# Scan tiles laid out anew, stores moved to GpSimd's queue, the prefill's first two blocks paired, attention issued behind the last scan

## The chip, the cores and the metric

The kernel runs on one NeuronCore of a Trainium2 chip. Such a core has five engines, each with its own queue of instructions in fixed order: TensorE (PE: matrix products; PEld is its loading of weights), VectorE (DVE), ScalarE (ACT), GpSimd (POOL) and SyncE (SP, which here only issues DMA transfers). Sixteen DMA engines move data between the chip's memory and SBUF, the on-chip memory of 128 partitions; products land in the eight banks of PSUM. Engines wait for one another through semaphores. The metric is the device time of one launch in microseconds, the median over runs.

## The reference, cut to what matters

One layer of a diffusion backbone works on 128 context tokens and 1024 latent tokens (9 blocks of 128), width 1024. Attention (8 query heads of 64, 2 key and value heads) and an mLSTM matrix memory (4 heads of 128, scanned forward and backward in chunks of 128) read one input projection and are merged by one output projection; a SwiGLU FFN of width 2816 follows. Everything is float32.

```python
def trunk_layer(x, mods, ...):
    sh1, sc1, g1, sh2, sc2, g2 = mods            # from silu(cond) @ w_ada
    h = rmsnorm(x, norm1_w) * (1 + sc1) + sh1
    aq, ak, av, mq, mk, mv, mo, mg = split(h @ w_in)
    attn_o = attention(rope(norm(aq)), keys, vals)
    hm = mlstm_bidir(mq, mk * DK ** -0.5, mv, gates, init_f, init_b)
    hm = rmsnorm(hm, mlstm_norm_w) * sigmoid(mo)
    mix = concatenate([attn_o, hm]) @ w_out      # rows 0-511: attn_o, 512-1023: hm
    x = x + g1 * mix
    h2 = rmsnorm(x, norm2_w) * (1 + sc2) + sh2
    return x + g2 * ((silu(h2 @ w_g) * (h2 @ w_u)) @ w_down)

# one step of the scan, per head and chunk
s   = (q @ k.T) * exp(log_d - m_t)
num = s @ v + inter * (q @ C);  den = s.sum(-1) + inter * (q @ n)
h   = num / max(abs(den), exp(-m_t))
```

## The kernel before, in words

**Stages.** The nine blocks form three groups of three (CB = 3). (1) Modulations, norm 1, keys, values, gates and the query projection. (2) For each of the four mLSTM heads: `head_project` (its projections) with `head_mlstm` (the scan) of the head before woven in, and with attention on block group 0. (3) The scan of the last head, with no projection left beside it. Woven into it are `first`, which is the output projection's attention half for blocks 0 to 2 (`attn_out_first`, its results x1a stored to the memory tensors `x1a_d`), `ada`, which is the last modulation (`ada_rest`, two rows stored to `g_d`), and attention on group 1. (4) `prefill`: the output projection's other half, hm times w_out's rows 512 to 1023, for all nine blocks, and norm 2 of group 0. (5) The FFN, group by group, with the rest of attention on groups 1 and 2 woven in.

**Products.** A float32 product is done as three products of a high and a low part. `load_piece` (line 139) loads a 512 KB piece of weights into `raw` (line 151), ScalarE casts the high part `whi` (line 152), VectorE subtracts for the low part `wlo` (line 137). `out_block` (line 1142) makes 512 output columns of one block from 12 products (lines 1147 to 1149); a "half" below is one such call, n = 0 or 1, with two pieces of weights.

**The scan of one block.** `weights` makes scores and decay factors (lines 843 to 851), then come the products with the states (866), with the values (873), the division (876 to 884), hm (886, 887), its squares (889), and GpSimd's products (890, 896). For the last head, each three blocks are normalised together and stored to `hm_d[0]`, `hm_d[1]`, `hm_d[2]` (line 898): the first by SyncE, the other two by ScalarE's queue.

**Attention.** A unit is the turn of one block's queries (line 1008 on), one head (scores 1035, maximum 1037, exponential 1038, high and low part 1041 and 1042, two transposing DMAs on SyncE's queue, 1044 and 1045), or the value products of a pair of heads (1059, 1060). Group 1 has 39 units.

**What sets the order.** The stages are generators. `weave(main, side, n_main, n_side)` advances a side generator by n_side / n_main per unit of the main one; `beside` advances several at rates of their own. The instructions so listed go through a scheduler that simulates the engines and picks for each queue the ready instruction of highest priority; `hot(n)` lifts priority by n places. So an attention unit can be issued somewhat earlier than where it is listed. The order on each queue is then fixed.

**Where tiles lie.** Pools are stacked from both ends of SBUF; within a pool the tags lie in the order of their first allocation. A tile of a later stage that lies over tiles of an earlier one waits for these tiles' last users, tile by tile. In stage 3 the stack from one end is the weight pool (`ipair`, `iraw`: 4 buffers of 4 KB per partition each), hT0 to hT2 (12 KB each, used by `attn_out_first` as x1a, gta, mxa), the gate tiles and `mlp` (the scan's tiles, in the order of the lines headed `for tag, shape, bufs, dt`). In stage 4 the same end holds raw (2 buffers), whi (5) and wlo (5), over ipair, iraw, hT0 and the start of hT1, then x1 of groups 0 and 1, then aTh and aTl. From the other end, below attention's pools, come `ft` (gl, gx, t2), `fp` and `xp` (gx_all, mx), over the upper part of `mlp`.

**Prefill before.** For each block b: `load_x1(b + 1)`, `load_hm(b + 1)` (into t2), four transposes of hm, cast and subtraction to mx, half 0, half 1, for b < 3 the sums of squares (`stats`), for 0 < b <= 3 norm 2 of block b - 1. Attention on group 1 is advanced by 0.35 per yield. All four weight pieces of the stage are asked for ahead of the loop by `out_pieces(1)`.

## Time and profile before

| | us |
|---|---|
| median of 3 runs (lowest, highest) | 1570.68 (1569.95, 1571.53) |
| the profiled execution's own time | 1568.19 |
| its span, first to last instruction | 1566.4 |
| TensorE busy | 1484.4 |
| VectorE busy | 1017.7 |
| ScalarE busy | 771.7 |
| GpSimd busy | 267.8 |

How to read it: the profile is of one execution. In rows of groups the fields are line, engine, operation, written tile <- read tiles, shapes, count, then busy us and mean ns of one, then the idle time just before these instructions and what ended it. In rows by stretch of time each engine's busy us stands with its count, then TensorE's granted clock as a share of full speed, the share of the DMA engines and GB/s. In rows of the chain or in order of time the first number is the start and the second the length, in us; in brackets stand the idle time before and its releaser. SPq and ACTq are transfers issued on SyncE's and ScalarE's queues. Ends of TensorE's products are modelled, so neighbours overlap in their lengths; the distance of starts is the better measure.

### The profile page before, as it was taken

To read this page: it belongs to the slowest core of one execution; us is meant where nothing else is said; L and a number is where in the kernel's file an instruction comes from. 1 tells how busy PE (TensorE), PEld (TensorE's weight loads), DVE (VectorE), ACT (ScalarE), POOL (GpSimd) and SP (SyncE) were. 2 spreads that over 40 slices of the span, in tenths; PEclk is the share of its full clock that TensorE was granted. 3 is DMA by queue.
4 is the path that set the end of the run, shared out by engine and by line. 5 is a ranking of instruction groups with operands and counts; after the bars stand their busy time and mean duration, and the time that the engine had idled before them with its cause. 6 is when DMAs were issued, how large, how long until landed. Compare 5 with 4: busy or idle time off the path is not lost.

```text
span 1566.4 us, 23369 instructions
## 1 busy us (share of the span) xinstructions
PE 1484.4 (95%) x8539; PEld 1244.8 (79%) x8539; DVE 1017.7 (65%) x2007; ACT 771.7 (49%) x1413; POOL 267.8 (17%) x354
## 2 busy tenths in 40 slices
PE   6899999999999689999999999999999999999997
PEld 3544567677766468898998989989898989999996
DVE  4878554837669576677555677878866585554554
ACT  4754465847656344545432444556552443323333
POOL 0213333322343242100110101000010101001110
PEclk9899999999999799999999999999999999999999
DMA  9564323523657748767554547878773545534441
GB/s 362 177 190 156 100 68 41 130 38 68 122 148 170 254 80 201 182 182 170 153 154 144 152 126 237 195 172 178 176 169 114 168 129 175 162 117 139 148 139 63
DMA packets 387881, 236.91 MB, mean 151 GB/s; under 512 B 170198, under 2 KB 346790, under 8 KB 387766
## 3 DMA queue, kind: packets, MB, share of 16 engines
q1 hardware_dynamic: 385110, 231.84, 54.2%
q10 hardware_dynamic: 2656, 3.58, 1.1%
q8 instruction: 67, 1.10, 0.3%
q14 instruction: 48, 0.39, 0.1%
HBM read 183.79 MB, written 13.26 MB: 126 GB/s over the span
## 4 chain that ended last, share of the span: by engine, by line
PE 80%; DVE 9%; ACT 4%; DMA 4%; issue 2%; POOL 1%; SPq 0%; ACTq 0%; DVEq 0%; POOLq 0%
PE mm L1316 12%; PE mm L1317 11%; PE mm L1315 11%; PE mm L1115 5%; PE mm L1116 5%; PE mm L1117 5%; PE S L1035 4%; PE wi L485 3%; PE wi L484 3%; PE wi L483 3%; PE mm L1147 2%; PE mm L1148 1%; PE mm L1149 1%; PE mm L116 1%; PE po L1060 1%
## 5 line engine op out<-in xcount | busy, mean ns | idle before, releaser
L152 ACT CAST whi<-raw 128x1024 fp32r<-128x1024 f32 (+1 forms) x216 | 221.9, 1027 | 415.1 <-PE mm L1316 148.8
L137 DVE TENSOR_TENSOR wlo<-raw,whi 128x1024 fp32r<-128x1024 f32 (+1 forms) x216 | 259.9, 1203 | 204.9 <-ACT whi L152 204.4
L1316 PE MATMUL mm<-aTl,whi 128*128 128x384 f32 x1056 | 355.7, 337 | 2.7 <-DVE aTl L137 2.7
L1317 PE MATMUL mm<-aTh,wlo 128*128 128x384 f32 x1056 | 354.3, 336 | 0.0
L1315 PE MATMUL mm<-aTh,whi 128*128 128x384 f32 x1056 | 353.3, 336 | 0.0
L137 POOL TENSOR_TENSOR hl<-tn,hl 128x384 fp32r<-128x384 f32 x66 | 84.1, 1275 | 840.0 <-ACT hl L1338 757.3
L1316 PEld LDWEIGHTS mm<-aTl,whi 128*128 128x128 f32 x1056 | 198.5, 188 | 3.9 <-DVE aTl L137 3.3
L1315 PEld LDWEIGHTS mm<-aTh,whi 128*128 128x128 f32 x1056 | 198.1, 188 | 0.6
L1317 PEld LDWEIGHTS mm<-aTh,wlo 128*128 128x128 f32 x1056 | 198.4, 188 | 0.0
L1116 PE MATMUL mm<-wlo,hl 128*128 128x512 f32 x372 | 145.7, 392 | 0.0
L1115 PE MATMUL mm<-whi,hl 128*128 128x512 f32 x372 | 144.3, 392 | 0.0
L1117 PE MATMUL mm<-whi,hl 128*128 128x512 f32 x372 | 143.4, 392 | 0.0
L483 PE MATMUL wi<-ipair,hT 128*128 128x384 f16 (+2 forms) x408 | 135.2, 334 | 2.0 <-ACT hT L507 1.2
L484 PE MATMUL wi<-ipair,hT 128*128 128x384 f16 (+2 forms) x408 | 135.2, 334 | 0.0
L485 PE MATMUL wi<-ipair,hT 128*128 128x384 f16 (+2 forms) x408 | 132.0, 335 | 1.0 <-DVE hT L137 1.0
L1042 DVE SCALAR_TENSOR_TENSOR pl<-pr,st,ph 128x1152 f16<-128x1152 f32 (+1 forms) x72 | 94.8, 1317 | 33.9 <-ACT ph L1041 32.5
L1041 ACT ACTIVATE ph<-pr,st 128x1152 f16<-128x1152 f32 (+1 forms) x72 | 83.8, 1164 | 27.2 <-issue 7.2
L1037 DVE TENSOR_REDUCE st<-S 128x1 f32<-128x1152 f32 (+1 forms) x72 | 88.8, 1233 | 12.5 <-PE S L1035 12.3
L1038 ACT ACTIVATE pr<-S,st 128x1152 f32<-128x1152 f32 (+1 forms) x72 | 81.3, 1129 | 31.7 <-DVE st L1037 28.0
L1035 PE MATMUL S<-kst,qT 128*128 128x384 f32 (+1 forms) x400 | 86.8, 347 | 5.0 <-ACT pr L1038 5.0
L1104 DVE TENSOR_TENSOR t<-mm,gl 128x512 f32<-128x512 f32 x102 | 68.9, 685 | 26.2 <-DMA gl<-g_d 12.5
L1117 PEld LDWEIGHTS mm<-whi,hl 128*128 128x128 f32 x372 | 69.9, 188 | 14.2
(381 smaller groups left out, 2525.0 us busy)
## 6 DMA issues: line engine op xcount, KB each, us to landing
raw<-in_w_gu_dram SPq DMA_DIRECT2D x132, 512.0 KB
raw<-in_w_down_dram SPq DMA_DIRECT2D x60, 512.0 KB
a<-in_w_ada_dram SPq DMA_DIRECT2D x24, 512.0 KB
gl<-g_d SPq DMA_DIRECT2D x36, 256.0 KB
aw<-in_w_ada_dram SPq DMA_DIRECT2D x16, 512.0 KB
iraw<-in_w_in_dram SPq DMA_DIRECT2D x32, 256.0 KB
raw<-in_w_out_dram SPq DMA_DIRECT2D x12, 512.0 KB
x<-in_x_sample_dram SPq DMA_DIRECT2D x11, 512.0 KB
```

The source lines that it names most:

```text
L137: (dve if eng == "dve" else pool).tensor_tensor(out=out, in0=full, in1=hi, op=ALU.subtract)
L152: nc.scalar.copy(hi[:, :n], raw[:, :n])
L483: mm(ps[:, :n], ah, wh[:, k % 2, c0 : c0 + n], start=(k == 0), stop=False)
L484: mm(ps[:, :n], ah, wl[:, k % 2, c0 : c0 + n], start=False, stop=False)
L485: mm(ps[:, :n], al, wh[:, k % 2, c0 : c0 + n], start=False, stop=(k == KD - 1))
L1035: mm(S[:, n, 0:w], qT[:, h, :], kst[kv][:, t, c0 + n * w : c0 + (n + 1) * w], start=(t == 0), stop=(t == 1))
L1115: mm(ps, ah, wh[:, k % 2, :], start=(k == 0), stop=False)
L1116: mm(ps, ah, wl[:, k % 2, :], start=False, stop=False)
L1117: mm(ps, al, wh[:, k % 2, :], start=False, stop=(k == nk - 1))
L1315: mm(ps, wh[:, k, :], th[:, k, :], start=(k == 0), stop=False)
L1316: mm(ps, wh[:, k, :], tl[:, k, :], start=False, stop=False)
L1317: mm(ps, wl[:, k, :], th[:, k, :], start=False, stop=(k == KD - 1))
```

## The change

1. The tags of `mlp` are laid out in another order: hm, ssh, nu, it, ... first, and c0f, c0b, cs and qTm last.
2. In `attn_out_first`, x1a and mxa change places (hT2 and hT0); w_out's high and low pieces take the four `iraw` buffers, and `ipair` takes ada's two weight buffers, the raw piece and ada's row.
3. Stores by GpSimd's queue: the last head's `hm_d[1]` and `hm_d[2]`, each as three stores of one block, the three `x1a_d` stores, and ada's two rows to `g_d`.
4. In the last scan ada is advanced at 0.8 and `first` at 0.55 per yield (0.5 and 0.35 before). Attention on group 1 is no longer in the chain woven there (0.14 per yield, 37 yields); it is made after it and first advanced by the prefill.
5. The prefill loads hm of blocks 0 and 1 first, into buffers `hmr` of its own, then two weight pieces (n = 0), the gates and gx_all; x1 of blocks 0 and 1 and the two pieces for n = 1 are issued on SyncE's queue after gx_all (`tc.issue_after`). Blocks 0 and 1 are transposed together, then come both halves 0, then both halves 1, each with its block's end; from block 2 on the order is as before. mx has 3 buffers instead of 2, and `xp` is laid out as gx_all, hmr, mx.

```diff
-    def ada_rest(ns, silp, new_a4, new_part, new_row, early=2):
+    def ada_rest(ns, silp, new_a4, new_part, new_row, early=2, store=dma):
...
-            dma(g_d[0 if n == 2 else 1, :, j * 512 : (j + 1) * 512], row)
+            store(g_d[0 if n == 2 else 1, :, j * 512 : (j + 1) * 512], row)
...
-    for tag, shape, bufs, dt in (("cs", [P, P + 1], CSB, F32), ("c0f", [P, P + 1], 2, F32), ("c0b", [P, P + 1], 1, F32), ("hm", [P, NB, P], 2, F32), ("ssh", [P, NB], 2, F32), ("nu", [P, 2, P + 1], 4, F32),
-                                 ("it", [P, 2, P + 1], 3, F32), ("dn", [P, 2], 3, F32), ("jkh", [P, P], 1, BF16), ("sd", [P, 2, P], 4, F32),
-                                 ("dt", [P, 2, P], 4, F32), ("so", [P, P], 9, F32), ("va", [P, P + 1], 9, F32), ("kT", [P, P], 9, F32),
-                                 ("th", [P, P], 1, F32), ("qTm", [P, CT], 2 * NCH, F32), ("wv", [P, 2, P + 1], 2, F32), ("kt", [P, P], 2, F32)):
+    for tag, shape, bufs, dt in (("hm", [P, NB, P], 2, F32), ("ssh", [P, NB], 2, F32), ("nu", [P, 2, P + 1], 4, F32), ("it", [P, 2, P + 1], 3, F32),
+                                 ("dn", [P, 2], 3, F32), ("jkh", [P, P], 1, BF16), ("sd", [P, 2, P], 4, F32), ("dt", [P, 2, P], 4, F32),
+                                 ("so", [P, P], 9, F32), ("va", [P, P + 1], 9, F32), ("kT", [P, P], 9, F32), ("th", [P, P], 1, F32),
+                                 ("kt", [P, P], 2, F32), ("wv", [P, 2, P + 1], 2, F32), ("c0f", [P, P + 1], 2, F32), ("c0b", [P, P + 1], 1, F32),
+                                 ("cs", [P, P + 1], CSB, F32), ("qTm", [P, CT], 2 * NCH, F32)):
...
-                    (nc.scalar.dma_start if h == NH - 1 and c > 0 else dma)(hm_d[c][:, h * P : (h + 1) * P].rearrange("(b p) n -> p b n", p=P), hm[:, c * CB : (c + 1) * CB, :])
+                    cols = hm_d[c][:, h * P : (h + 1) * P]
+                    if alone and c > 0:
+                        for k in range(CB):
+                            nc.gpsimd.dma_start(cols[k * P : (k + 1) * P], hm[:, c * CB + k, :])
+                    else:
+                        dma(cols.rearrange("(b p) n -> p b n", p=P), hm[:, c * CB : (c + 1) * CB, :])
...
-        ahead = load_hm(0)
-        load_x1(0)
-        ws = out_pieces(1)
+        hms = [load_hm(0), load_hm(1)]
+        ws = [out_pieces(1, 0)]
         gs = out_gates()
-        gx_all = xp.tile([P, D], F32, name="gx_all")
-        dma(gx_all, g_d[0, 0:1, :].to_broadcast([P, D]))
+        gx_all = xp.tile([P, D], F32, name="gx_all", tag="gx_all")
+        with tc.issue_after(dma(gx_all, g_d[0, 0:1, :].to_broadcast([P, D])).ins):
+            load_x1(0)
+            load_x1(1)
+            ws.append(out_pieces(1, 1))
...
+        for b in range(2):
+            mix(b)
+            yield
+        for b in range(2):
+            half(b, 0)
+            yield
+        for b in range(2):
+            load_x1(b + 2)
+            half(b, 1)
+            yield
+            yield from end(b)
+        for b in range(2, NB):
+            load_x1(b + 2)
+            mix(b)
+            yield
+            for n in range(2):
+                half(b, n)
+                yield
+            yield from end(b)
...
-        x1 = hTp.tile([P, CB, D], F32, name="x1a", tag="hT0")
+        x1 = hTp.tile([P, CB, D], F32, name="x1a", tag="hT2")
         gt = hTp.tile([P, 6, 512], F32, name="gta", tag="hT1")
-        mx = hTp.tile([P, CB, NQ, P], F32R, name="mxa", tag="hT2")
-        ip = [wp.tile([P, 1024], F32R if i < 2 else F32, name=nm("ip"), tag="ipair", bufs=4) for i in range(4)]
-        ir = [wp.tile([P, 1024], F32R if i < 2 else F32, name=nm("ir"), tag="iraw", bufs=4) for i in range(4)]
+        mx = hTp.tile([P, CB, NQ, P], F32R, name="mxa", tag="hT0")
...
+        his, los = (ir[0], ir[1]), (ir[2], ir[3])
...
-                        dma(x1a_d[i], x1[:, i])
+                        nc.gpsimd.dma_start(x1a_d[i], x1[:, i])
...
-    oT = []
-    att = chain(att, attention(1, oT, set()))
-    weave(scan, beside((ada, 0.5), (first, 0.35), (att, 0.14)), 37, 37)
+    weave(scan, beside((ada, 0.8), (first, 0.55), (att, 0.14)), 37, 37)
     while len(done) < CB:
         next(att)
+    emit(att)
+    oT = []
+    att = attention(1, oT, set())
     emit(first)
```

`mix`, `half` and `end` are the former loop's three parts under names of their own; `out_pieces(half, n)` now returns the two pieces of one n.

More of the change, by code (lines that the diff above doesn't have):

```diff
@@ L1121, in three_blocks, with out_pieces @@
                 done(i, ps)
-    def out_pieces(half, own=None):
-        ws = []
-        for n in range(2):
-            pieces = []
-            for j in range(2):
-                r0 = half * 512 + 2 * j * P
-                rows = w_out[r0 : r0 + 2 * P, n * 512 : (n + 1) * 512].rearrange("(a p) n -> p a n", p=P)
-                pieces.append(load_piece([(full_view, rows)], (2, 512), raw=own and own[2], own=own))
-                own = None
-            ws.append(pieces)
-        return ws
+    def out_pieces(half, n):
+        pieces = []
+        for j in range(2):
+            r0 = half * 512 + 2 * j * P
+            rows = w_out[r0 : r0 + 2 * P, n * 512 : (n + 1) * 512].rearrange("(a p) n -> p a n", p=P)
+            pieces.append(load_piece([(full_view, rows)], (2, 512)))
+        return pieces
     def out_gates():
@@ L1202, in prefill @@
-            if c == 0:
+            cs = slice(n * 512, (n + 1) * 512)
+            ps = out_block(ws, n, *mixed[b])
+            g = gx[n] if b == 0 else gs[n]
+            if c < 2:
+                add_gated(x1s[c][i], ps, g, n, pool)
+            else:
+                xt = t2()
+                dma(xt, xrow(b)[:, cs])
+                t = t2()
+                dve.tensor_tensor(out=t, in0=ps, in1=g, op=ALU.mult)
+                pool.tensor_tensor(out=xt, in0=xt, in1=t, op=ALU.add)
+                dma(x1_d[i][:, cs], xt)
```

47 lines of the change are left out of this document (20 added, 27 removed).

## Prediction

> **What bounds the kernel now.** I read the page first (busy shares, the 40 slices), then the busy time by stretch around the one slice in which TensorE falls to 6 tenths, then the chain in order of time through that place, then what each queue issued there.
>
> ```profile
> span 1566.4 us, 23369 instructions
> PE 1484.4 (95%) x8539; PEld 1244.8 (79%) x8539; DVE 1017.7 (65%) x2007; ACT 771.7 (49%) x1413; POOL 267.8 (17%) x354
> PE   6899999999999689999999999999999999999997
> PE 80%; DVE 9%; ACT 4%; DMA 4%; issue 2%; POOL 1%; SPq 0%; ACTq 0%; DVEq 0%; POOLq 0%
> ```
>
> TensorE is busy 95% of the span and carries 80% of the chain. So what counts is where it idles or runs at a lowered clock; work that is only carried to another place costs its own length there and saves it here. The 14th slice (509 to 548 us) is the worst after the start. It is the passage from the last mLSTM scan to the prefill, which is what the diff touches.
>
> ```profile
> core 0: us, PE busy (x) PEld busy (x) DVE busy (x) ACT busy (x) POOL busy (x), PEclk, DMA share, GB/s
> 450.00:460.00 10.00, 7.05 (x42) 5.33 (x40) 7.46 (x21) 8.01 (x24) 6.93 (x9) 0.83 0.41 114
> 480.00:500.00 20.00, 18.79 (x124) 14.70 (x123) 19.19 (x58) 15.27 (x34) 6.40 (x7) 1.00 0.83 163
> 500.00:532.00 32.00, 17.94 (x75) 12.63 (x74) 19.53 (x43) 9.50 (x16) 6.25 (x6) 0.73 0.81 248
> 502.00:514.30 12.30, 8.38 (x46) 5.27 (x44) 10.56 (x29) 3.38 (x9) 5.20 (x5) 0.86 0.79 197
> 523.80:532.00 8.20, 7.53 (x20) 5.79 (x21) 3.34 (x4) 2.02 (x3) 0.00 (x0) 0.54 0.91 343
> 541.00:560.00 19.00, 12.87 (x74) 10.02 (x75) 15.62 (x42) 11.91 (x22) 7.09 (x5) 1.00 0.41 89
> 600.00:660.00 60.00, 56.24 (x325) 50.00 (x323) 39.56 (x52) 30.36 (x39) 12.44 (x9) 1.00 0.84 209
> ```
>
> TensorE's loss in this passage: idle 20 - 18.79 = 1.2 us and 32 - 17.94 = 14.1 us. To it comes work done at a lowered clock: 8.38 x (1 - 0.86) = 1.2 us and 7.53 x (1 - 0.54) = 3.5 us. Together **20.0 us**, the most that closing this hole alone can return. VectorE is full (19.19 of 20) before it. By the slices TensorE is at 9 tenths or more again from the 16th on (587 us), so anything moved there is paid there.
>
> ```profile
> 508.70 1.29 SPq L1044
> 510.10 1.29 SPq L1045
> 511.44 5.24 DMA raw<-in_w_out_dram
> 519.44 4.29 DMA t<-hm_d
> 455.85 0.90 PE L785 MATMUL mm<-wv,kt 128*128 128x258 f32 x2 [2.10 <-POOL wv L783]
> 498.95 0.61 PE L873 MATMUL wi<-va,sd 128*128 128x129 f32 x4
> 503.19 1.31 PE L1035 MATMUL S<-kst,qT 128*128 128x384 f32 x6
> 523.78 1.11 PE L116 MATMUL mm<-ident,t 128*128 128x128 f32 x4 [9.47 <-DMA t<-hm_d]
> ```
>
> The chain says why. The scan's last products run at 498.95, but SyncE's queue must first issue two attention transposes (508.70, 510.10), which wait for a softmax of attention on block group 1 that was woven into the scan. Only then come three weight loads, the third of them waiting for a buffer, and behind these, at 519.44, the load of the first hm block. TensorE waits 9.47 us for that load, and after it runs at clock 0.54.
>
> **The change, part by part.** *Attention behind the scan.* The scan yields 37 times; at 0.14 that drew five units of attention on group 1: the q turn and four heads. These now come with the prefill. The prefill draws as many units as before, so five more are left for the FFN.
>
> ```profile
> L1035 PE MATMUL S<-kst,qT 128*128 128x384 f32 x36 | 7.7, 350 | 0.0
> L116 PE MATMUL mm<-ident,qr 128*128 128x128 f32 x4 | 0.6, 272 | 0.0
> L1042 DVE SCALAR_TENSOR_TENSOR pl<-pr,st,ph 128x1152 f16<-128x1152 f32 x5 | 7.0, 1404 | 0.0
> L849 ACT ACTIVATE dt<-mm,QT 128x128 f32<-128x128 f32 x18 | 5.7, 365 | 3.6 <-PE mm L846 3.5
> L869 ACT ACTIVATE it<-wi,QT 128x129 f32<-128x129 f32 x16 | 5.1, 366 | 2.1 <-PE wi L866 2.1
> L886 ACT ACTIVATE hm<-nu,dn 128x128 f32<-128x128 f32 x9 | 3.5, 403 | 3.8 <-DVE dn L884 3.8
> L889 ACT ACTIVATE jkh<-hm 128x128 bf16<-128x128 f32 x10 | 3.1, 312 | 4.9 <-DVE hm L887 4.9
> L889 ACT ACTIVATION_READ_ACCUMULATOR jkh<-hm 128x1 f32 x10 | 1.9, 193 | 0.0
> 468.99 0.60 PE L866 MATMUL wi<-cs,qT 128*128 128x129 f32 x4
> 470.21 0.27 PE L846 MATMUL mm<-NM,selb 128*128 128x256 bf16 x1
> ```
>
> TensorE's part of the five units is 4 x 1.3 + 0.6 = 5.8 us; it is moved, not saved, and counts in neither direction. VectorE loses at least 4 x 1.40 = 5.6 us (L1042 alone) in the scan, where it was full. SyncE loses eight transposes of about 1.3 us, which will stand between weight loads of the FFN. What does cost: in 600 to 660 TensorE idles 60 - 56.24 = 3.8 us while the 23 units then left begin (39 less 5 and 11); if all of that is attention's, five more are **+0.8 us** (0 to 2).
>
> *Side work at 0.8 and 0.55.* The last modulation and the first half of the out projection now end after some 24 of the 37 yields instead of at the end. That frees the buffers under the new weights early, but the last 13 yields, 3.25 blocks, are scan alone. A block's products take 468.99 to 470.48, 1.5 us of TensorE; ScalarE needs 2 x 0.365 + 2 x 0.366 + 0.40 + 0.31 + 0.19 = 2.4 us. At ScalarE's pace TensorE idles 3.25 x 0.9 = **2.9 us**. Ends: 0, if prefill's transposes and halves fill in; 10.7 us at the old pace (from the last projection product at 455.85 to 498.95, 43.1 us for nine blocks, 4.8 each, 3.25 x 3.3). I take ScalarE's, since the old pace held attention and projection work too.
>
> *Layout.* Worked out from the tile sizes, the prefill's hm buffers now lie on kT, done with the last score product, no longer on t2 and rsqrt space; the low weight halves lie on mxa instead of on x1a, so they wait for the last projection product, not for x1a's stores. In exchange the x1 tile lies on x1a and so waits for all three of x1a's stores, and gx_all lies on va, free only after the scan's last product. This is what lets the hm load and the first two weight pieces be issued before the scan ends. Its price is in the next part.
>
> *Prefill paired, n=1 weights behind gx_all.* On SyncE the gx_all load must go out first, then two x1 loads, then the two n=1 pieces; attention's transposes queue behind them. None can start before va is free.
>
> ```profile
> 520.96 0.59 SPq L151 DMA_DIRECT2D raw<-in_w_out_dram  x1
> 522.11 0.65 SPq L1173 DMA_DIRECT2D gx_all<-g_d  x1
> 522.81 0.64 SPq L1166 DMA_DIRECT2D x<-x1a_d  x1
> 529.50 1.04 ACT L152 CAST whi<-raw 128x1024 fp32r<-128x1024 f32 x1 [3.98 <-DMA raw<-in_w_out_dram]
> 530.57 1.23 DVE L137 TENSOR_TENSOR wlo<-raw,whi 128x1024 fp32r<-128x1024 f32 x1 [4.34 <-ACT whi L152]
> 535.14 0.50 PE L1147 MATMUL mm<-whi,mx 128*128 128x512 f32 x1 [0.68 <-ACT mx L1184]
> 540.48 0.39 PE L1149 MATMUL mm<-whi,mx 128*128 128x512 f32 x1
> ```
>
> From the scan's last product to the first n=1 half: 0.65 + 2 x 0.64 + 0.59 issue, 8.5 landing (520.96 to 529.50), 1.04 cast, 1.23 subtract = 13.3 us. Cover on TensorE: the two n=0 halves, as long as block 1's two (535.14 to 540.87, 5.7 us), two transposed blocks (four transposes each as for the q turn, 1.2), and the q turn with two hoisted heads (3.2): 10.1 us. A new wait of **3.2 us** is left. Ends: 0 with the faster landing (511.44 plus 5.24 us), 6.4 without the heads. If the cover is gone altogether it is 13.3.
>
> *Clock.* A gap of 2.10 us at 455.85 lies in the stretch with clock 0.83: 7.05 x 0.17 = **1.2 us** for one more such gap (0 to 3.5, the loss after the long one). The Trainium skill, "TensorE: Matmul & The Clock Gate", Part 1, says that the clock halves after an idle window of about 3.4 us. By that, gaps of 3 us could go free and the sum would be 1.2 us better. The trace shows a lowered clock around 2.10 us.
>
> *Stores on GpSimd's queue.* Eleven: six pieces of hm in place of two stores on ScalarE's queue, three of x1a and two gate rows in place of five on SyncE's. The trace has none from GpSimd, so no price.
>
> ```profile
> 511.07 0.38 ACTq L898 DMA_DIRECT2D hm_d<-hm  x1
> 602.44 2.06 DMA x_d<-t
> ```
>
> The nearest issue row is 0.38 us; GpSimd is busy 6.25 us of 32, so 11 x 0.38 = 4.2 us hides, and I take nothing. The upper end is a store that holds the queue until it has landed, 2.06 us each. Behind it stand the hm products, the x1a sums and prefill's x1 sums, and SyncE's x1 load waits for the three x1a stores. A gain is possible too, as SyncE loses waits for GpSimd's sums; it stands in the hole already.
>
> **The sum.** 20.0 recovered, minus 2.9, 3.2, 1.2 and 0.8 = 8.1 left over: 11.9 us less. The profiled execution took 1568.19 us (span 1566.4 and 1.8 around it), so 1556.3 for it. The median of the runs, 1570.68, is 2.5 above that execution: **1559 us**. The likeliest's own range: the terms' ends hardly come together, so half of what they allow, 8.1 / 2 down and (7.8 + 3.2 + 2.3 + 1.2) / 2 up: 1555 to 1566.
>
> **The rivals.**
> *All of it closes* (15 in 100): the scheduler lays prefill halves into the scan's tail and the weights land in time. All 20 us go: 1551, and 1548 where half of the prefill's idle at 541 to 560 (19 - 12.87 = 6.1 us) goes too. For it: by the code the hm blocks 0 to 2 are stored when six blocks of the scan are still to come. Against: gx_all's wait on va.
>
> *The hole moves* (15 in 100): SyncE's queue, in order, waits at gx_all or x1, and the n=1 weights come 6 us later still. 11.9 - 6 = 5.9 us less: 1565. For it: the third and fourth weight loads cost just such waits now.
>
> *Attention was free filler* (7 in 100): the scan keeps its old pace to the end, 10.7 us idle in place of 2.9. 11.9 - 7.8 = 4.1 less, and with a second lowered clock (1.2) 2.9 less: 1568, no measurable change. Against: the chain's own steps at 508.70 and 510.10 are attention's.
>
> *GpSimd's queue becomes the bound* (13 in 100), the slower case: each store holds the queue for its landing. Three x1a stores, two rows and three hm pieces stand there in the last 25 us: 8 x 2.06 = 16.5 us, plus the sums between. The x1 load goes out that much later, with the n=1 weights behind it on SyncE. From 11.9 us of such delay the gain is gone; at 16.5 it is 4.6 slower: 1575. For it: VectorE and GpSimd are both at work there. Against: by the new rates x1a's sums end after some 20 of the 37 yields, and the time up to the scan's end may swallow most.
> The Trainium skill, "SBUF — State Buffer", "A bandwidth-pool intuition that's wrong", speaks against the change here: GpSimd writes the descriptors of its own stores and is locked out during some VectorE operations, with a store-like transfer of 620 ns becoming 3100. By an estimate from that figure eight stores would hold 25 us and the kernel would be 13 us slower. No trace here shows it.
>
> **How the numbers follow.** The likeliest has 50 in 100. A change under 0.2% (3.1 us) can't be told from none. Faster: 50 + 15 + 15 = 80; within 0.2%: 7; slower: 13. The range leaves out the far part of the first rival (some 8) and the far half of the last (6): 1549 to 1575.
>
> **What would show it.** Right: the wait for hm gone, SyncE issuing hm and the first weights before the scan's last product, no attention transposes between them, TensorE's clock near 1 through the passage, first FFN products about 18 us earlier than 611.9 (11.9 and the 5.8 moved).
> ```profile
> L1315 PE MATMUL mm<-aTh,whi x1056: 331/334/423, 611.9 to 1538.6; 128*128 128x384 f32 x176
> ```
> Wrong: a wait of over 10 us before the n=1 halves, GpSimd holding x1 sums, or TensorE idle within the scan in place of attention.

## The result, and the profile after

The changed kernel takes 1575.28 us (median of 18 runs, 1571.37 to 1582.65) against 1569.89 us of the kernel before in the same series: a ratio of 1.0037, 95% interval 1.0027 to 1.0046. It is slower, where I had forecast 1559 us and faster. Its profiled execution took 1571.5 us (span 1569.7), which is 3.8 below its own median; the one of before lies 1.7 below its median of 1569.89. So the two traces differ by 3.3 us and the medians by 5.4: some 2 us of the loss are not in this trace.

Lines have moved: 866 is now 867, 873 is 874, 898 is 902 and 904, 1147 to 1149 are 1149 to 1151, 1250 is 1278, 1161 is 1163, 1166 is 1168, 1035 is 1041, 869 is 870, 851 is 852, 1294 is 1322, 1315 is 1343.

From the page of the changed kernel: TensorE's 40 slices, and the chain's shares by engine.

```profile
PE   6799999999987699999999999999999999999997
...
PE 77%; DVE 9%; DMA 5%; ACT 5%; issue 2%; POOL 1%; SPq 0%; ACTq 0%; DVEq 0%; POOLq 0%
```

The dent in the slices has not gone. It was a 6 and an 8 (the 14th and 15th slice); it is now an 8, a 7 and a 6 (the 12th to the 14th), so it is longer and begins two slices earlier. Busy time by stretch, first of the kernel before, then of the changed one, shows this in us:

```profile
440.00:480.00 40.00, 36.85 (x246) 27.41 (x244) 27.77 (x74) 24.07 (x70) 16.87 (x23) 0.96 0.47 139
480.00:541.00 61.00, 44.92 (x233) 33.58 (x231) 43.73 (x112) 27.57 (x53) 16.52 (x16) 0.86 0.84 237
541.00:600.00 59.00, 50.01 (x261) 40.29 (x262) 43.32 (x92) 31.57 (x50) 21.94 (x16) 1.00 0.50 100
600.00:660.00 60.00, 56.24 (x325) 50.00 (x323) 39.56 (x52) 30.36 (x39) 12.44 (x9) 1.00 0.84 209
```

```profile
440.00:480.00 40.00, 32.38 (x204) 22.87 (x204) 20.05 (x62) 16.30 (x51) 12.46 (x20) 0.91 0.55 174
480.00:541.00 61.00, 38.91 (x210) 30.17 (x208) 40.54 (x117) 25.46 (x59) 25.11 (x29) 0.85 0.65 214
541.00:600.00 59.00, 53.91 (x277) 45.06 (x278) 44.62 (x86) 32.51 (x50) 22.63 (x16) 0.92 0.52 113
600.00:660.00 60.00, 58.72 (x324) 54.20 (x323) 33.96 (x45) 26.32 (x34) 10.49 (x8) 1.00 0.67 190
```

TensorE (first busy column) loses 36.85 - 32.38 = 4.5 us in 440 to 480 and 44.92 - 38.91 = 6.0 in 480 to 541, and takes back 3.9 and 2.5 behind that: 4.1 us less work by 660. All of the 10.5 lost ahead of 541 is idle time; up to 5.8 of it stands where attention's products stood, which were moved away on purpose, and the rest is new. The granted clock is lower too, 0.91 for 0.96 and 0.92 for 1.00.

What TensorE waited for in the passage (changed kernel, 440 to 700; total, times, longest):

```profile
PE mm L116 <- DMA hmr<-hm_d: 12.5, 1, 12.5
PE mm L116 <- ACT y L1322: 6.7, 1, 6.7
PE mm L116 <- ACT it L870: 3.9, 1, 3.9
PE mm L844 <- DVE sd L852: 2.6, 1, 2.6
```

The wait for hm, 9.47 us before, is 12.5. Three others are new or longer: 6.7 for norm 2's y (1.49 before the same transposes in the old trace), and 3.9 and 2.6 at the start of the last scan. The chain in order of time says what held hm (changed kernel):

```profile
502.35 0.60 POOL hm_d L902
502.95 1.57 issue
504.52 0.54 POOL hm_d L902
505.06 1.58 issue
506.64 0.54 POOL hm_d L902
507.18 1.57 issue
508.75 0.53 POOL x1a_d L1278
509.28 2.49 DMA g_d<-ip
511.86 4.16 DMA raw<-in_w_out_dram
```

GpSimd issues a store in 0.5 to 0.6 us, then stands 1.57 us before the next: 2.1 us a store, far from the 0.38 us row on which I had counted. The last gate row's store waits behind three stores of hm and one of x1a until 509.28. And SyncE waits for that row, since the second weight piece is loaded over it. SyncE's waits from 480 to 530 divide this wait, and SyncE's queue (start, length) shows what stood behind it:

```profile
SPq L151 <- DVE ip L453: 11.1, 1, 11.1
SPq L151 <- DMA g_d<-ip: 7.6, 1, 7.6
```
```profile
492.60 19.62 SPq L151 DMA_DIRECT2D raw<-in_w_out_dram  x2
512.27 0.93 SPq L1163 DMA_DIRECT2D hmr<-hm_d  x2
516.08 2.73 SPq L151 DMA_DIRECT2D raw<-in_w_out_dram  x2
```

The first piece goes out at 492.6, the second only at 511.86, and the hm loads, whose data was stored long before, stand behind it in the same queue. Of the second piece's wait 11.1 us pass until VectorE has finished the row (line 453), and 7.6 until its store has been issued and has landed. So the store on GpSimd's queue is the smaller part of this wait, and the larger is that ada's last row is finished so late.

### The profile page after: what moved, and what is told of

The parts are those of the page before. It is cut to its first block, busy times and chain, and to the rows that moved or that the text cites. A ratio compares the mean times of both kernels' runs of the same rounds, so it can differ in the third digit from the quotient of the medians.

```text
span 1569.7 us, 23407 instructions
## 1 busy us (share of the span) xinstructions
PE 1482.2 (94%) x8539; PEld 1248.4 (80%) x8539; DVE 1017.8 (65%) x2007; ACT 771.8 (49%) x1413; POOL 273.1 (17%) x365
## 4 chain that ended last, share of the span: by engine, by line
PE 77%; DVE 9%; DMA 5%; ACT 5%; issue 2%; POOL 1%; SPq 0%; ACTq 0%; DVEq 0%; POOLq 0%
PE mm L1344 11%; PE mm L1345 11%; PE mm L1343 11%; PE mm L1121 5%; PE mm L1122 5%; PE mm L1123 5%; PE S L1041 4%; PE wi L485 3%; PE wi L483 3%; PE wi L484 3%; PE po L1066 1%; PE mm L1151 1%; PE po L1065 1%; PE mm L1150 1%; PE mm L1149 1%
## 5 line engine op out<-in xcount | busy, mean ns | idle before, releaser
L1048 DVE SCALAR_TENSOR_TENSOR pl<-pr,st,ph 128x1152 f16<-128x1152 f32 (+1 forms) x72 | 98.7, 1371 | 32.3 <-ACT ph L1047 32.0
```

## The experiments

Medians and ratios are to the kernel before of the same series (1569.77 to 1570.18 us).

| run | edit | median, us | ratio (95%) |
|---|---|---|---|
| changed kernel | | 1575.28 | 1.0037 (1.0027 to 1.0046) |
| e1_row_apart | gate row in a buffer of its own | 1574.29 | 1.0028 (1.0015 to 1.0041) |
| e2_row_on_sync | gate rows stored by SyncE | 1574.22 | 1.0028 (1.0017 to 1.0038) |
| e3_ring | 2048 B for GpSimd's descriptors | 1571.80 | 1.0012 (1.0000 to 1.0024) |
| f1_row_ring | e1 and e3 (1024 B) | 1570.66 | 1.0005 (0.9994 to 1.0015) |
| e4_stores_back | all stores on their old queues | 1570.64 | 1.0000 (0.9991 to 1.0009) |
| h1_swap_only | projection's buffers as before | 1572.56 | 1.0015 (1.0002 to 1.0029) |
| f2_back_swap | e4 and h1 | 1568.33 | 0.9990 (0.9979 to 1.0001) |
| f3_ring_swap | e3 and h1 | 1565.01 | 0.9968 (0.9958 to 0.9977) |
| h2_hm2_gpsimd | f2, hm's last store on GpSimd | 1562.81 | 0.9959 (0.9942 to 0.9977) |
| e5_unpaired | blocks 0 and 1 not paired | 1577.74 | 1.0054 (1.0039 to 1.0069) |
| f6_ring_swap_unpair | f3, not paired | 1568.89 | 0.9992 (0.9982 to 1.0003) |
| e6_att_in | attention in the scan | 1577.11 | 1.0054 (1.0038 to 1.0069) |
| c2_row_att | e1 and e6 | 1578.79 | 1.0057 (1.0045 to 1.0069) |
| f7_att_in_scan | f3, attention in the scan | 1569.05 | 0.9998 (0.9985 to 1.0011) |
| g1_old_rates | f3, rates 0.5 and 0.35 | 1567.50 | 0.9980 (0.9968 to 0.9992) |
| g2_mid_rates | f3, rates 0.8 and 0.35 | 1568.01 | 0.9987 (0.9973 to 1.0000) |
| b1_stores_only | before, only the stores moved | 1576.84 | 1.0042 (1.0029 to 1.0056) |
| b2_stores_ring | b1, 2048 B | 1577.64 | 1.0045 (1.0030 to 1.0059) |

The intervals put a difference between two runs clear of noise from some 2.5 us on (an estimate: two half widths of about 1.8 us, added as squares). So the 1.0, 1.1, 1.8 and 2.3 us below stand for no clear change, and 2.5 to 2.7 are at the edge.

My theory (A) was that the held stores on GpSimd's queue cost the time, by way of the gate row; the rivals (B) that attention and the pairing cost it, and (C) that freeing the row only moves the wait.

**The gate row alone.** The new buffer lies at the end of `mlp`.
```diff
-lambda: ip[3][0:2, 512:1024]
+lambda: mlp.tile([2, 512], F32, name=nm("row5"), tag="row5", bufs=1)
```


> The changed kernel (1575.3 us), with one edit: the last gate row gets a buffer of its own, so the second weight load no longer overwrites it and no longer waits for its store on GpSimd's queue. Theory A (the store of that row, behind three hm stores and an x1a store, holds SyncE's second weight load to 511.9 and with it both hm loads at 512.3): the second weight load and the hm loads are issued by about 504, the wait for hm falls from 12.5 us to 4 to 5 us, and 6 to 8 us go: 1567 to 1569. Rival B (the time is lost in 450 to 480 and 532 to 541, by attention gone from the scan and by the pairing, and the hm loads would wait anyway, for buffers that the scan holds): the hm wait stays over 9 us and the time within 3 us of 1575. Rival C (the delay moves on: gx_all and x1 wait for GpSimd's stores, so the n=1 weights come late): hm wait under 6 us, a new wait of over 5 us in the n=1 halves, time over 1571.

1574.29 us, 1.0 less than the changed kernel. The hm loads went out at 504.31 as expected and the wait for hm fell to 1.8 us, but the time did not follow. Rival C holds, though its new wait is 4.1 us and not over 5, as TensorE's and SyncE's waits and SyncE's rows of this run show:

```profile
PE mm L1149 <- ACT whi L152: 4.1, 1, 4.1
...
PE mm L116 <- DMA hmr<-hm_d: 1.8, 1, 1.8
```
```profile
SPq L1168 <- DMA x1a_d<-x1a: 11.1, 1, 11.1
```
```profile
518.70 0.80 SPq L1168 DMA_DIRECT2D x<-x1a_d  x2
519.59 0.90 SPq L151 DMA_DIRECT2D raw<-in_w_out_dram  x2
```

The x1 tile lies on x1a, so its load waits 11.1 us for x1a's third store, which stands behind the same three stores of hm; the n=1 weights follow it on SyncE at 519.59, later than in the changed kernel (516.08). The new wait and the scan's last product, at 506.8 in place of 504.0, can account for 6.9 of the 10.7 us that the wait for hm lost; the rest I have not followed.

**The gate rows on SyncE.**
```diff
-lambda: ip[3][0:2, 512:1024], 1, nc.gpsimd.dma_start)
+lambda: ip[3][0:2, 512:1024], 1)
```


> The changed kernel, with only the last modulation's two gate rows stored by SyncE's queue again (hm and x1a stay on GpSimd's). Theory A: the row's store no longer stands behind the hm stores, is issued at about 504 and lands 2 us later; the second weight load starts at 506 to 507 in place of 511.9, the hm wait falls by 5 us to about 7.5, the time to about 1570. Rival B: no change of over 2 us.

1574.22 us: a miss by 4 us, and for the same reason. The second piece and the hm loads went out by 507.4, the x1 loads not before 520.1.

**More space for GpSimd's descriptors.**
```diff
-dynamic_dma_scratch_size=256)
+dynamic_dma_scratch_size=2048)
```


> The changed kernel, with 2048 in place of 256 bytes a partition for the descriptors of GpSimd's queue. Theory A1 (a store waits 1.57 us at issue because the descriptors of the one before it still fill that space): the stores of hm go out 0.6 us apart in place of 2.1, the gate row's store is issued at about 505 in place of 509.3, the second weight load at about 507, and the time falls by 4 to 5 us to 1570 to 1571. Rival A2 (GpSimd's queue holds each store until it has landed, whatever the space): stores stay 2.1 us apart and the time at 1575.

1571.80 us, 3.5 less, and the hold is gone. GpSimd's rows in this run:

```profile
506.62 1.66 POOL L902 DMA_DIRECT2D hm_d<-hm  x3
508.28 0.54 POOL L1278 DMA_DIRECT2D x1a_d<-x1a  x1
508.90 0.52 POOL L454 DMA_DIRECT2D g_d<-ip  x1
```

Five stores follow each other 0.5 to 0.6 us apart, where the first three gaps of the changed kernel were 2.1. A1 holds as far as the two runs can tell: a store waits until the space holds its descriptors. It fits with this that the row, two partitions wide, followed x1a's store after 0.53 us in the changed kernel, too. The times expected for the row and the second piece did not come: in this execution the row was finished later (its store at 508.90), SyncE still waited 12.2 us for it, and the hm loads went out at 511.80, while the wait for hm was 7.6 us. The Trainium skill, "SBUF — State Buffer", "A bandwidth-pool intuition that's wrong", puts a slow GpSimd transfer down to VectorE locking out the writer of descriptors. The trace does not agree here: VectorE was no less busy in this run (third busy column, 480 to 541, against 40.54 of the changed kernel), and no hold was left.

```profile
480.00:541.00 61.00, 41.61 (x218) 31.09 (x217) 43.23 (x123) 26.17 (x61) 25.98 (x30) 0.88 0.66 216
```

In size the hold is near what the Trainium skill, "DMA: Bandwidth & Descriptors", "Anatomy of one DMA — SWDGE (gpsimd) path", gives for one whole transfer: by its fit, 2.0 us and the bytes by 436 GB/s, an estimate of 2.15 us for 64 KB. The changed kernel's chain has 2.17 and 2.12 between the three stores of hm. With other transfers under way it went further: the last two pieces of hm in the changed kernel, from 512 to 524, went out 5.2 and 5.6 us after the one before, at a DMA share of 0.93, against 0.08 from 502 to 509.

**Row and space together.** The first and the third edit, with 1024 bytes.


> The changed kernel with both mendings of GpSimd's queue at once: the gate row in a buffer of its own, and 1024 in place of 256 bytes a partition for the queue's descriptors. The row's buffer alone moved the hm loads 7.9 us forward and gave 1.0 us of time (1574.3), because the x1 loads then waited for x1a's last store, held back behind the hm stores, until 518.7; the space alone gave 3.5 us (1571.8). Theory M (one wait behind the other: with both gone the x1 loads go out by about 512 and the n=1 weights by 513): hm wait under 4 us and 1567 to 1570. Rival N (the n=1 weights land 10 us after their issue whatever is done, and the norm's wait for y of 6.7 us stays): 1571 to 1573.

1570.66 us, 1.1 below the space alone, a little under N's range. The wait for hm (1.9) was as M has it, and GpSimd held nothing. But x1a's last store, issued at 509.70, now runs beside the other transfers; x1 waits 7.0 us for its landing and goes out at 517.8. So M fell on the x1 loads.

**All stores back.**
```diff
-for k in range(CB):
-    nc.gpsimd.dma_start(cols[k * P : (k + 1) * P], hm[:, c * CB + k, :])
+nc.scalar.dma_start(cols.rearrange("(b p) n -> p b n", p=P), hm[:, c * CB : (c + 1) * CB, :])
...
-nc.gpsimd.dma_start(x1a_d[i], x1[:, i])
+dma(x1a_d[i], x1[:, i])
```
and the gate rows as in e2.


> The changed kernel with all stores on the queues they had before (hm's last pieces on ScalarE's, x1a and the gate rows on SyncE's). Theory A: the hm wait falls to 7 us or less, GpSimd has no wait for issue left, and the time is 1567 to 1570. Rival D (SyncE's queue then waits for GpSimd's x1a sums ahead of the weight loads): the second weight load stays at over 510 and the time at 1574 to 1577. Rival B: within 2 us of 1575.

1570.64 us, a shade over theory A's range, and the kernel before within 0.1%. So the stores' return takes back 4.6 us, the whole loss that can be measured. It also says that all the rest of the change, on which I had counted for 11.9 us, comes to nothing by itself. The wait for hm is still 7.7 us here, over the 7 expected.

**The stores alone, on the kernel before.** Without and with the larger space.


> The kernel before (1569.9 us), with only the stores of the change: two gate rows, three x1a pieces and six hm pieces on GpSimd's queue. My prediction's step: hidden, 1569.9 within 1 us. Theory A: they hold the queue 2 us each here too; the kernel before has no weight load behind the gate row in GpSimd's order that lies ahead of the hm load, so the loss is smaller than in the changed kernel, 0 to 3 us: 1570 to 1573. Rival: a gain of 1 to 3 us, since SyncE no longer waits for GpSimd's sums.

> The kernel before with only the stores moved to GpSimd's queue (1576.8 us), and 2048 bytes for that queue's descriptors. If the space is what holds the stores here too: no wait for issue on GpSimd, and 1569 to 1571, the kernel before within 0.1%. If something else in the move costs (GpSimd's own time at each store, or SyncE's waits for its stores): 1574 to 1577.

1576.84 and 1577.64 us, 6.9 and 7.7 slower. I had expected 0 to 3, and that the space would mend it. It does not, so here the cause is, at least in part, another. SyncE's and GpSimd's rows of b2:

```profile
515.39 9.69 SPq L151 DMA_DIRECT2D raw<-in_w_out_dram  x4
525.13 0.46 SPq L1166 DMA_DIRECT2D t<-hm_d  x1
```
```profile
513.53 1.69 POOL L901 DMA_DIRECT2D hm_d<-hm  x3 [0.29 <-POOL hm L896]
```

GpSimd holds nothing in b2 (in b1 it does). But the kernel before asks for three weight pieces and then for hm, at 519.44; in b1 and b2 the scheduler, which plans all queues again, puts the fourth piece first, too, and hm goes out at 522.0 and 525.1. Part of the delay was there earlier: the last two transposes of attention end at 512.9 and 515.3 in place of 511.4. What moved these I have not settled, so the loss of b1 and b2 is explained only in part.

**The projection's weight buffers.** In the changed kernel the projection's raw weights lie in the group of buffers (`ipair`) that the last head's projection still reads. h1 undoes only this; f2 also has e4's stores, f3 e3's space. The edit, with the buffers' types left out:
```diff
-his, los = (ir[0], ir[1]), (ir[2], ir[3])
+his, los = (ip[0], ip[1]), (ir[0], ir[1])
-return (ip[0], ip[1])[turn[0] % 2]
+return ip[2 + turn[0] % 2]
-lambda: ip[3][:, 0:512], lambda: ip[3][0:2, 512:1024]
+lambda: ir[3][:, 0:512], lambda: ir[3][0:2, 512:1024]
-raw=ip[2], own=(his[j], los[j])
+raw=ir[2], own=(his[j], los[j])
```


> The changed kernel (1575.3 us) with only the projection's weight buffers as before the change; the small space for GpSimd's descriptors stays. The second weight load then no longer lies on the gate row, so its wait for GpSimd's queue goes with the exchange: hm loads by about 502, no hm wait. The x1 loads still wait for x1a's last store behind three held hm stores, to 515 or later. If the buffers alone are worth what they were with the larger space (5.7 to 6.8 us): 1568.5 to 1569.6. If the hold of the x1 loads takes it back, as in the run with the row apart: 1571 to 1574.

> The kernel with all stores on their old queues (1570.6 us), and the projection's weight buffers as before the change (raw and low halves in the second group of four buffers, where the change has them in the first group, which the last head's projection still reads). Theory L (the layout delays the projection's first weight load to 445.8, ScalarE's queue stands 3.2 to 3.8 us at its cast, and TensorE idles 3.3 to 3.9 and 2.6 us for what stands behind): both waits under 1 us, TensorE's busy time in 440 to 480 back up by 3 to 6 us from 33.3, and 1565 to 1568. Rival (VectorE is the bound of the scan, and the time comes back as idle behind it): waits gone, but the time within 1.5 us of 1570.6.

> The changed kernel, all its stores on GpSimd's queue, with 2048 bytes for that queue's descriptors and the projection's weight buffers as before the change (so the second weight load also no longer lies on the gate row). Theory L and M together: no wait for issue on GpSimd, no cast waiting at 451, hm wait under 4 us: 1562 to 1567, faster than both kernels. Rival N (the n=1 weights and the norm set the pace whatever comes before): 1568 to 1571.

1572.56 (2.7 less than the changed kernel), 1568.33 (2.3 less than e4) and 1565.01 us (6.8 less than e3, 7.6 less than h1). f3 beats the kernel before by 0.32%, as expected; h1 fell in the poorer of its two ranges, and f2 just missed theory L's, with no more TensorE work in 440 to 480 (33.2 us). With enough space for descriptors the stores on GpSimd's queue are thus 3.3 us better than on their old queues (f3 against f2), not worse. The mechanism shows in ScalarE's rows, first of the changed kernel, then of f3:

```profile
451.70 1.04 ACT L152 CAST ir<-ip 128x1024 fp32r<-128x1024 f32 x1 [3.81 <-DMA ip<-in_w_out_dram]
```
```profile
448.30 1.03 ACT L152 CAST ip<-ir 128x1024 fp32r<-128x1024 f32 x1
458.72 1.04 ACT L152 CAST ip<-ir 128x1024 fp32r<-128x1024 f32 x1 [2.19 <-DMA ir<-in_w_out_dram]
```

In the changed kernel the output projection's first load waits for the last head's products and goes out at 445.83 (at 367.2 in the kernel before, 368.9 in f3); ScalarE stands 3.81 us at the cast, and behind it stand the scan's first factors, for which TensorE waits 3.9. In f3 that wait is gone, but a second cast now waits 2.19, and TensorE's wait for sd is 4.9 in place of 2.6: so theory L was right on the first wait and wrong on the second. h1 shows that neither mending does alone: its x1 loads wait 11.8 us for x1a's store and go out at 518.2. Only with both does the path come free, in f3 (its profiled execution, 1568.98 us, is the slowest of its runs, so its waits are, if anything, too long):

```profile
493.15 8.15 SPq L151 DMA_DIRECT2D raw<-in_w_out_dram  x2
501.36 1.06 SPq L1163 DMA_DIRECT2D hmr<-hm_d  x2
...
512.32 1.71 SPq L1168 DMA_DIRECT2D x<-x1a_d  x2
```

This is what I had forecast for SyncE, 10.9 us ahead of the changed kernel (512.27) and ahead of the scan's last product, and TensorE has no wait for hm left.

**hm's last store.** In f2 (and e4) the n=1 weight loads are issued late, as SyncE's waits of f2 say:
```profile
SPq L151 <- DMA hm_d<-hm: 7.4, 1, 7.4
```
They neither read nor overwrite hm. As I read the program as built, transfers of SyncE and ScalarE take turns on a few completion counters, and this load gets the one of hm's last store, so it waits for that store first. No trace shows these counters; what a trace can show is whether the wait goes with the store. The edit puts that store alone on GpSimd, with 2048 bytes.
```diff
-if alone and c > 0:
-    nc.scalar.dma_start(cols.rearrange("(b p) n -> p b n", p=P), hm[:, c * CB : (c + 1) * CB, :])
+if alone and c == 2:
+    for k in range(CB):
+        nc.gpsimd.dma_start(cols[k * P : (k + 1) * P], hm[:, c * CB + k, :])
 else:
-    dma(cols.rearrange("(b p) n -> p b n", p=P), hm[:, c * CB : (c + 1) * CB, :])
+    (nc.scalar.dma_start if alone and c > 0 else dma)(cols.rearrange("(b p) n -> p b n", p=P), hm[:, c * CB : (c + 1) * CB, :])
```


> The kernel with all stores on their old queues and the buffers as before (1568.3 us), but hm's last three pieces on GpSimd's queue, with 2048 bytes for its descriptors. If the n=1 weight loads wait only because they share a completion counter with ScalarE's store of hm's last pieces: they are issued at about 509 in place of 516, and 1563 to 1566. If the wait is of another origin (a buffer): they stay at 515 to 517 and the time within 1.5 us of 1568.

1562.81 us, 5.5 less than f2 and the fastest of all: 0.41% below the kernel before, 12.5 us below the changed one. SyncE's row, then TensorE's waits:

```profile
506.77 1.82 SPq L151 DMA_DIRECT2D raw<-in_w_out_dram  x2
```
```profile
PE mm L116 <- ACT y L1322: 10.0, 2, 7.8
PE mm L116 <- DMA hmr<-hm_d: 6.6, 1, 6.6
PE mm L844 <- DVE sd L852: 4.9, 1, 4.9
```

The n=1 weights go out 9.2 us earlier than in f2 (515.97), and the wait for them is under 1 us. So the wait does go with the store; that a counter is the link stays a reading of the program. What is left of the passage are mainly the three waits above.

**The pairing.** Undone in the changed kernel and in f3.
```diff
-for b in range(2):
-    mix(b)
-    yield
...
-for b in range(2, NB):
+for b in range(NB):
```


> The changed kernel without the pairing: the prefill's blocks 0 and 1 one after the other, n=0 and n=1 of block 0 before block 1. Theory P (the pairing lets norm 2 of block 0 end in a wait of its own, the 6.7 us for y at 541.7): that wait falls under 2 us, but the first n=1 half comes one block earlier than the n=1 weights and waits for them 2 to 6 us; the time is within 3 us of 1575. Rival Q (the pairing costs its whole 6.7 us, and the n=1 weights are there): 1568 to 1570. Rival R (the pairing is worth more than its wait): 1578 to 1582.

> As the run before (descriptor space and weight buffers mended), with the prefill's blocks one after the other. In the changed kernel as it stands the pairing gave 2.5 us (1577.7 without it). If the pairing covers the n=1 weights: 2 to 5 us slower than the run before. If its exposed norm (the 6.7 us for y) outweighs that once the weights come earlier: 1 to 4 us faster than it.

1577.74 and 1568.89 us: the pairing is worth 2.5 and 3.9 us. The exposed norm did not go with it (y still 6.0 and 5.8 us), so neither the mending of P nor that of f6's second case came. The pairing covers the n=1 weights, as its first case has it.

**Attention.** Woven into the scan again, in the changed kernel, with the row apart, and in f3.
```diff
-weave(scan, beside((ada, 0.8), (first, 0.55), (att, 0.14)), 37, 37)
...
-emit(att)
-oT = []
-att = attention(1, oT, set())
+oT = []
+att = chain(att, attention(1, oT, set()))
+weave(scan, beside((ada, 0.8), (first, 0.55), (att, 0.14)), 37, 37)
```


> The changed kernel with attention on group 1 woven into the scan at 0.14 again. Theory F (attention's products filled TensorE's idle time in 450 to 480, where the changed kernel idles 4.7 + 2.9 us in place of 3.0 + 0.2): 4 to 5 us of busy time come back there, against SyncE's transposes ahead of the second weight load, which waits for the gate row's store anyway: 1570 to 1573. Rival G (the transposes wait for the softmax and put off the loads again, as before the change): the hm wait grows by 3 us or more and the time stays at 1574 to 1578.

> The changed kernel with the gate row in a buffer of its own and attention woven into the scan at 0.14 again, both at once. If the two losses are separate (theory A and theory F together): 1575.3 less 6 to 8 less 4 to 5, so 1562 to 1566, better than the kernel before by 4 to 8 us. If attention's transposes on SyncE's queue take back what the row's buffer gives (rival G): 1567 to 1571.

> The faster kernel (1565.0 us) with attention on group 1 woven into the scan again. In the changed kernel as it stands this cost 1.8 us, with eight transposes on SyncE ahead of the hm loads and VectorE's softmax in a full scan. Theory G (the transposes hold SyncE, as before the change): hm loads after 510, 1567 to 1571. If attention is filler that TensorE lacks in the scan: 1560 to 1563.

1577.11, 1578.79 (neither of its two expectations) and 1569.05 us: attention behind the scan is worth 1.8 (in the changed kernel, not clear of noise) to 4.5 us. Theory F (filler) fell: TensorE's busy time in 440 to 480 rose by 0.7 and 1.7 us in e6 and f7, but the transposes put SyncE's hm loads off to 517.4 and 513.0. In e6 they also pushed all six pieces of hm behind each other on GpSimd, up to 543.5, with prefill's sums behind them; TensorE waited 16.8 us for y, in two waits.

**The rates of the side work.** In f3, both old (g1), then the projection's 0.35 alone with 0.8 for the modulation (g2).
```diff
-beside((ada, 0.8), (first, 0.55), (att, 0.14))
+beside((ada, 0.5), (first, 0.35), (att, 0.14))
```


> The faster kernel (descriptor space and weight buffers mended, 1565.0 us), with the side work at its old rates, 0.5 and 0.35. Theory S (at 0.55 the projection's second weights are cast before they have landed, and the scan's first blocks wait 4.9 us behind ScalarE): that wait falls under 2 us, TensorE's busy time in 440 to 480 rises by 3 to 5 us from 34.0; against it the weight buffers come free at the scan's end, the hm loads go out 3 to 6 us later, and the gate row later still: 1565 to 1569. If the early end of the side work is not needed: 1560 to 1563.

> The same kernel with the last modulation at 0.8 and the projection at its old 0.35. The scan's first blocks lose their wait as in the run before; the gate row is done early, but the projection's products end with the scan, so the first weight pieces and x1a's stores are as late as there: 1564 to 1568. Under 1563 if only the row had to be early.

1567.50 and 1568.01 us: the higher rates are worth 2.5 to 3.0 us, as the times expected have it, but theory S fell. The wait for sd stays 4.4 and 4.7 us, so the rates are not its cause. It was 0.8 in the kernel before; with attention back in the scan it is still 3.6 us (f7), so attention is not the whole cause either. The new order of the scan's tiles was not undone in any run, and its part stays open.

## Why the prediction was wrong

*What bounds the kernel.* Right in the main: the passage from the last scan to the prefill decides, and a queue in order, SyncE's, sets it. f3 and h2 gained their 5 and 7 us there. But I read only the softmax as what held the two transposes. In the chain of the kernel before, ada's row stands just ahead of them: VectorE finishes it at 507.99 (line 453), SyncE stores it at 508.41, and the first transpose follows at 508.70. The second one's softmax part ended at 509.73, so both held the queue. Ada's late row held it after the change again.

*Stores on GpSimd's queue: "4.2 us hides, and I take nothing".* **This step failed.** It took the issue for the whole price. A store held the queue for 2.1 us, and for 5.2 and 5.6 beside other transfers, and two loads on SyncE hung on it: the second weight piece (through the gate row) and x1 (through x1a). Putting the stores back gave 4.6 us, more space for descriptors 3.5. My rival of that name had nearly the right price, 2.06 us a store, but named only the x1 load; the gate row came first, and x1 showed itself when the row was freed. That its total, 1575, is the measured time is luck: it sets 16.5 us of delay against a gain of 11.9, while the runs show no gain (e4) and 4.6 us of loss.

*Side work at 0.8 and 0.55: it ends "after some 24 of the 37 yields", which "frees the buffers under the new weights early".* **Failed.** The projection's products run to 498.40 and ada's last to 500.06, beside the scan's last ones (before: 501.92 and 502.24):

```profile
498.40 0.39 PE L1151 MATMUL mm<-ir,mxa 128*128 128x512 f32 x1
500.06 1.02 PE L450 MATMUL mm<-ip,strip_sel 128*2 128x512 f32 x2
```

So the last row was finished only at 504.1, 11.1 us after SyncE was ready for the piece that lies on it, and x1a's last sum at 502.2. Why the side work ended so late stays open; its first load came late (next item).

*Layout: "This is what lets the hm load and the first two weight pieces be issued before the scan ends".* **Failed** for the second piece and so for hm. I had placed x1, hm and gx_all, and left out that ada's row lies in the same group of buffers as the pieces. The exchange also had a price that I had not listed at all, at the other end of the scan: the output projection's first load waits for the products of the last head's projection. From the first product with values to the last the scan takes 38.6 us before and 39.5 after, no less, though attention was taken out of it; and it begins 3.8 us later:

```profile
L873 PE MATMUL wi<-va,sd x36: 271/275/377, 460.7 to 499.3; 128*128 128x129 f32 x36
```
```profile
L874 PE MATMUL wi<-va,sd x36: 273/275/423, 464.5 to 504.0; 128*128 128x129 f32 x36
```

The late start goes with the exchange in every trace: the first product with values starts between 464.4 and 469.0 in the nine runs that have it, and between 461.1 and 463.9 in the eight that undo it. With enough space for descriptors, undoing the exchange gave 6.8 us (e3 to f3), and 5.7 if the row is taken out of it (f1 to f3).

*Scan's tail without filler, 2.9 us.* Near in size, but by luck: TensorE idles 20 - 18.27 = 1.7 us in 480 to 500 (1.2 before) and 1.4 before the last product, yet the tail was not the scan alone, as the side work ran beside it to the end.

```profile
480.00:500.00 20.00, 18.27 (x124) 14.21 (x122) 14.78 (x50) 9.73 (x29) 9.09 (x11) 1.00 0.44 143
```
```profile
503.55 0.71 PE L874 MATMUL wi<-va,sd 128*128 128x129 f32 x4 [1.37 <-DVE nu L877]
```

*n=1 weights, 3.2 us.* Hidden in the changed kernel, since the n=0 halves came late themselves. Where they came early it was 4.1 (e1) and 6.2 us (h1), and the cause was x1's wait for x1a's store, not gx_all's for va; in h2 it is under 1.

*The wait for norm 2.* Missing from my sum: norm 2 of block 0 used to run beside the halves of block 1 with a wait of 1.5 us, and now TensorE waits 6.7 us for it. I took this for the pairing's price, but without the pairing 6.0 and 5.8 us are left (e5, f6), so its cause stays open. The pairing itself gained 2.5 to 3.9 us.

*Clock, 1.2 us.* Too small. The hole stayed, and the waits at 450 to 480 came on top; the granted clock went from 0.96 to 0.91 in 440 to 480 and from 1.00 to 0.92 in 541 to 600. By these rows, at 32.4 and 53.9 us busy, an estimate of 1.6 + 4.3 us.

*Attention moved, +0.8 us in the FFN.* Not borne out: TensorE's idle time in 600 to 660 fell from 3.8 to 60 - 58.72 = 1.3 us. My marker was a bad one: the first FFN product came at 605.3, 6.6 us earlier, while the kernel got slower, as products of the prefill had slipped behind it; the last of these starts at 611.6, against 611.7 before.

*The rivals.* That all closes fell: even h2 keeps waits of 6.6 and 7.8 us. That attention was free filler fell with f7. That the hole moves to x1 is what e1 and h1 show.

So the mechanism of the gain was right in part: f3 and h2 lie 4.8 and 7.1 us below the kernel before, of 11.9 forecast, and f3 issues hm and the first weights as foreseen, but waits of 7.4 us for y and 4.9 for sd, which were not in the sum, take much of it back. The change as made lost the gain to two things that I had priced at nothing, the held stores and the exchange of buffers.

## What to carry to other kernels

A store moved to another engine's queue is not priced by its issue: list the transfers that follow it in that queue, and every load elsewhere that waits for one of them, and ask for the space that its descriptors need. When buffers change places, go through both ends: who waits at the end for what now lies there, and who waits at the beginning. And undo each part alone before judging the whole: here one half of a change hid that the rest was worth 0.3% (f3), and 0.4% with one store moved (h2).

## What the runs showed of the hardware that I had not expected

- With 256 bytes a partition for descriptors GpSimd's stores of 64 KB went out 2.1 us apart, and 5.2 and 5.6 us apart where other transfers filled the DMA engines (changed kernel); with 1024 or 2048 bytes 0.55 us apart (f1, e3).
- A load on SyncE's queue waited 7.4 us for a store of ScalarE's queue whose data it neither reads nor overwrites (f2); with that store on GpSimd's queue the wait was gone and the time 5.5 us lower (h2).
- The same move of stores cost the kernel before 7.7 us with no hold on GpSimd (b2); part of it is that another queue was planned in another order, the rest is open.
